# A two-layer hybrid trunk on one core: order of the gating work, place of the rotary tables, split scaling of probabilities, and the last transposes of a gating group

## The chip, the cores and the metric

The kernel runs on one core of one Trainium2 chip. The metric is device time in microseconds (us) for one execution; the median over several runs counts, and lower is better. TensorE multiplies matrices, VectorE (DVE in the profile) and ScalarE (ACT) do elementwise work, GpSimd (POOL) does elementwise work too and issues some transfers, and SyncE (SP) issues most transfers.

## The reference

The reference is a decoder trunk over 1024 tokens of width 1024, in float32, with two layers:

- Layer 0 mixes tokens with latent attention: a down projection to 704 columns (384 for queries, 256 for keys and values, 64 for a shared rotary key), norms, 8 heads with a plain part of 128 and a rotary part of 64, causal softmax, an output projection.
- Layer 1 mixes tokens with a chunked gating unit: `z = gelu(hn @ w_in)` is cut into halves u and v of 2048 columns; v gets a layer norm; within each block of 128 tokens and each of 8 groups of 256 columns, `sv = tril(w_s) @ v + b_s`; then `y = u * sv` and the mixer returns `y @ w_out`.
- After each mixer comes a feed-forward part (width 4096, squared relu) and a gated input embedding, both added to the residual stream.

## The kernel before

**Numbers.** Each float32 operand X of a product is split into a rounded part Xh (a copy, on ACT) and the rest Xl = X - Xh (on DVE); a product is Wh*Xh + Wh*Xl + Wl*Xh, three matmuls that accumulate in PSUM. `split` (L110 to L112) makes such a pair. Every matmul of the helper `mm` is recorded at L65.

**Order.** The program is written as one stream. A planner at build time turns it into one queue for each engine: it goes through a model of the engines' times and, where an engine is free in the model and the next instruction of the program is not ready in it, takes a later one that is. On the chip each queue then runs in its fixed order, and an instruction that must wait holds up all that stand behind it on its engine. `tc.issue_after(ins)` keeps the instructions of a block behind `ins` on the same engine.

**Start (L1002 to L1319).** x comes in blocks of 128 tokens. `block_x` transposes a block on TensorE; `block_lat` multiplies it by the down weights, eight k steps of six matmuls, and the first two blocks run interleaved. The weights arrive by transfer, one slice for each k; `down_weight(k)` makes their rounded part on ACT (L1065) and the rest on DVE (L1066) just before step k of block 0. At the end of block 0 (L1130) `rotary()` calls `rope_tables` (L1461 to L1490): six DVE instructions reduce the angles (L1468 to L1472), ACT forms a magnitude and two sines (L1475 to L1477) behind a load of another function table, DVE forms the sine and cosine tables from them (three instructions at L1478 to L1480, eight at L1486 to L1489), and ACT loads the table of logarithm and exponential again (L1288). `rotary()` then also transposes the remaining gains (L1289) and forms one product of gains (L1290). After block_lat, ACT squares the latent rows (L1136), `rsqrt_small` takes reciprocal roots behind the table load, DVE scales the rows into `lats` (L1141 to L1143), and `block_c` transposes `lats` on TensorE (L1151, tile `cp`).

**Attention (L1321 to L1458).** The work is cut into 32 units, a head and a pair of query blocks. `scores` (L1348) computes a row block of n = 128 to 1024 keys, DVE finds the maximum, ACT the exponentials with their sum (L1373), DVE the reciprocal (L1375), and POOL multiplies the n probabilities by it in one instruction (L1376). `turn_p` (L1379) transposes the probabilities in groups of 256 keys (L1388 to L1393, tile `pt`), and `values` (L1399) multiplies them with the values.

**Gating unit (L782 to L928).** First all v columns are computed, their statistics taken, and v parked in memory. Then four groups `gp` of 512 columns follow. In a group, for each of the 8 token blocks b: `unit(b)` computes u (24 matmuls, tile `up`) and ACT applies gelu; `prep(b)` brings v back in pairs of blocks (tile `vr`, one of four buffers shared with weights), normalizes it on DVE (L884), multiplies and adds the norm's gains on POOL (L885, L886) and splits it into `vhl`, of which there is one buffer in a group; `spatial(b)` multiplies by the spatial weights (tile `sv`) and DVE forms y in place of u (L908, two instructions); `turn_y(b)` transposes y (L914, tile `yp`) and splits it into `yh`, `yl`. The loop at L918 runs spatial(b-2), unit(b), prep(b-1), turn_y(b-2). Then `down_slice` (L656) multiplies the group's y by its 512 rows of `w_out` (tile `go`) and adds to the residual stream (L665). With `seq=True` its first output tile (j = 0) is computed for tokens 0 to 511 first and for tokens 512 to 1023 after; the others alternate between the two halves. Block 7 is in the second half.

## Time and profile before

| | |
|---|---|
| median of 3 runs | 2653.01 us (2651.12 to 2656.77) |
| the profiled execution, its own time | 2655.07 us |
| its span, first to last instruction | 2653.3 us |
| mean granted TensorE clock | 0.995 |
| DVE busy | 1480.3 us (56%) |
| ACT busy | 1040.1 us (39%) |
| POOL busy | 322.8 us (12%) |

The profile gives, for each engine, its busy time; views of it list which instructions an engine waited for and how long, the instructions in order of time, groups of equal instructions, and the granted clock of a stretch. "Idle before" an instruction is the time in which its engine did nothing just before it, with the instruction whose end ended it.

### The profile page before, as it was taken

What the parts mean: (1) busy time and instruction counts of PE and PEld (TensorE: products, weight loads), DVE (VectorE), ACT (ScalarE), POOL (GpSimd) and SP (SyncE); (2) the same over time, 40 slices, a digit from 0 to 9 for tenths busy, and PEclk for the clock granted to TensorE, in tenths of its full rate; (3) what the DMA queues carried; (4) which work ended last, traced back from release to release, by engine and by line L of the source; (5) the groups of instructions that cost most, each with busy time, mean ns of one, the idle gap of its engine ahead of it and who ended that gap; (6) DMA issues with size and microseconds to landing.
All of it is one profiled execution on the core that took longest, in us unless ns stands there. A gap on an engine that the chain in (4) does not pass through costs nothing. (4 is left out here: it accounts for less than half of the span.)

```text
span 2653.3 us, 33181 instructions
## 1 busy us (share of the span) xinstructions
PE 2595.6 (98%) x12736; PEld 2193.9 (83%) x12736; DVE 1480.3 (56%) x2396; ACT 1040.1 (39%) x2109; POOL 322.8 (12%) x460
## 2 busy tenths in 40 slices
PE   7999999999999999999999999999999999999999
PEld 7988888878888888888888787888788888888887
DVE  5677775886565434375522545336966654444641
ACT  4576773654443212164522312214644441221430
POOL 4544431000000000001211433030000000000000
PEclk9999999999999999999999999999999999999999
DMA  5200002233345323233232312212333362332220
GB/s 163 71 8 21 25 25 88 96 119 104 127 151 190 115 68 111 64 100 90 86 111 95 101 39 88 77 43 96 98 125 111 120 228 97 112 111 64 80 76 36
DMA packets 211341, 247.41 MB, mean 93 GB/s; under 512 B 9792, under 2 KB 159872, under 8 KB 211184
## 3 DMA queue, kind: packets, MB, share of 16 engines
q1 hardware_dynamic: 206368, 230.21, 26.9%
q0 software_dynamic: 4816, 15.10, 1.9%
q8 instruction: 100, 1.64, 0.3%
q14 instruction: 57, 0.47, 0.1%
HBM read 186.55 MB, written 58.72 MB: 92 GB/s over the span
## 5 line engine op out<-in xcount | busy, mean ns | idle before, releaser
L111 ACT CAST wh<-raw 128x1024 fp32r<-128x1024 f32 x96 | 100.9, 1051 | 390.8 <-PE f0d L65 130.3
L665 DVE TENSOR_TENSOR f0h<-f0d,f0h 128x512 f32<-128x512 f32 (+1 forms) x84 | 70.4, 866 | 166.0 <-PE f0d L65 166.0
L665 DVE TENSOR_TENSOR f1h<-f1d,f1h 128x512 f32<-128x512 f32 (+1 forms) x84 | 70.4, 865 | 157.5 <-PE f1d L65 157.5
L112 DVE TENSOR_TENSOR wl<-raw,wh 128x1024 fp32r<-128x1024 f32 x96 | 117.8, 1227 | 56.5 <-ACT wh L111 50.3
L744 POOL TENSOR_TENSOR f0h<-sig,f0h 128x512 f32<-128x512 f32 x16 | 21.9, 1388 | 846.1 <-DVE sig L743 827.4
L65 PE MATMUL go<-yl,wh 128*128 128x512 f32 x256 | 84.3, 395 | 2.7 <-DVE yl L112 2.7
L824 DVE BATCH_NORM_STATS2 vst<-vg 128x6 f32<-128x512 f32 (+1 forms) x40 | 23.3, 586 | 113.5 <-ACT vg L823 113.4
L65 PE MATMUL go<-yh,wh 128*128 128x512 f32 x256 | 84.6, 395 | 0.0
L65 PE MATMUL go<-yh,wl 128*128 128x512 f32 x256 | 83.3, 392 | 0.0
L894 ACT ACTIVATE u<-up,n_r 128x512 f32<-128x512 f32 x32 | 22.0, 687 | 155.4 <-PE up L65 155.2
L665 DVE TENSOR_TENSOR f0h<-go,f0h 128x512 f32<-128x512 f32 (+1 forms) x52 | 40.4, 809 | 63.6 <-PE go L65 63.6
L65 PE MATMUL s<-kT,q 128*128 128x512 f32 (+5 forms) x288 | 72.8, 355 | 2.4 <-DVE q L112 1.8
L823 ACT ACTIVATE vg<-vp,n_r 128x512 f32<-128x512 f32 (+1 forms) x40 | 24.0, 603 | 122.9 <-PE vp L65 121.5
L65 PE MATMUL av<-pt,v 128*128 128x256 f32 (+1 forms) x480 | 64.1, 284 | 5.2 <-DVE sm L1375 2.7
L65 PEld LDWEIGHTS av<-pt,v 128*128 128x128 f32 x480 | 59.9, 191 | 8.1 <-issue 3.7
L1376 POOL TENSOR_SCALAR p<-p,sm 128x128 f32<-128x128 f32 (+3 forms) x64 | 49.2, 770 | 86.8 <-DVE sm L1375 55.3
L65 PEld LDWEIGHTS go<-yl,wh 128*128 128x128 f32 x256 | 48.4, 189 | 13.3 <-DVE yl L112 3.8
L65 PE MATMUL f1d<-f_ah,wh 128*128 128x512 f32 x192 | 59.3, 390 | 0.0
L65 PE MATMUL f0d<-f_ah,wh 128*128 128x512 f32 x192 | 59.2, 390 | 0.0
L65 PE MATMUL f0d<-f_al,wh 128*128 128x512 f32 x192 | 59.2, 389 | 0.0
L65 PE MATMUL f1d<-f_al,wh 128*128 128x512 f32 x192 | 59.2, 389 | 0.0
L65 PE MATMUL f1d<-f_ah,wl 128*128 128x512 f32 x192 | 59.1, 389 | 0.0
(5412 smaller groups left out, 8029.2 us busy)
## 6 DMA issues: line engine op xcount, KB each, us to landing
raw<-in_ffn_w_down_dram SPq DMA_DIRECT2D x56, 512.0 KB, 3.6
f0ar<-f_apark SPq DMA_DIRECT2D x32, 512.0 KB, 3.5
f1ar<-f_apark SPq DMA_DIRECT2D x32, 512.0 KB, 3.4
raw<-in_ffn_w_down_dram SPq DMA_DIRECT2D x32, 256.0 KB, 3.0
raw<-in_ple_w_gate_dram SPq DMA_DIRECT2D x16, 512.0 KB, 4.1
vr<-vpark SPq DMA_DIRECT2D x16, 512.0 KB, 4.4
raw<-in_gmlp_w_out_dram SPq DMA_DIRECT2D x16, 512.0 KB, 3.5
vpark<-vg POOLq DMA_DIRECT2D x24, 256.0 KB, 2.3
```

What stands on the lines that cost most here:

```text
L65: PE.matmul(o, l, r, start=start, stop=stop)
L111: S.copy(hi, src)
L112: V.tensor_tensor(lo, src, f32(hi), op=ALU.subtract)
L665: V.tensor_tensor(h[j][:, c], u, h[j][:, c], op=ALU.add)
L744: G.tensor_tensor(h[j][:, cs], sg, h[j][:, cs], op=ALU.add)
L823: last = S.activation(t, o, AF.Gelu_apprx_tanh, scale=nrm.r[:, b:b + 1])
L824: V.bn_stats(vst[:, b, cc], t)
L894: S.activation(us[b][:, b % 2], o, AF.Gelu_apprx_tanh, scale=r[:, b:b + 1])
L1376: G.tensor_scalar(pr_[:, :n], pr_[:, :n], sm[:, 2:3], 1.0, op0=ALU.mult, op1=ALU.mult)
```

## The change

Four things change.

- **Gating order.** The normalization of v (L884) of block b is kept, on DVE, behind the second half of the split of block b-2 (of block 0 where b is 1), and that of block 0 behind the last split of y of the group before.
- **The last y transposes.** `turn_y(7)` leaves the loop. `down_slice` computes its first two output tiles together in the new `gemm_pair`: both for tokens 0 to 511, then both for tokens 512 to 1023; the four transposes of block 7 are put behind matmul 21 of the 24 of the first half, and kept behind it on TensorE.
- **Rotary tables.** `rotary()` is called at step k = 1 of block 0 rather than k = 7; the transposition of the gains stays at k = 7 as `later_gains()`.
- **Probabilities.** The POOL instruction at L1376 becomes two where n is over 512: columns 0 to 511, and the rest.

```diff
-        PE.matmul(o, l, r, start=start, stop=stop)
+        return PE.matmul(o, l, r, start=start, stop=stop).ins
...
     def split(hi, lo, src):
         S.copy(hi, src)
-        V.tensor_tensor(lo, src, f32(hi), op=ALU.subtract)
+        return V.tensor_tensor(lo, src, f32(hi), op=ALU.subtract).ins
+    @contextmanager
+    def behind(ins):
+        if ins is None:
+            yield
+        else:
+            with tc.issue_after(ins):
+                yield
     def load_block(w, k0, f0, nk=4, nf=256):
         cnt[0] += 1
...
                 for c in cset:
                     mm(acc[c], wl, rhs[k][c][0], False, k == nk - 1)
         return units
+    def gemm_pair(blocks, rhs, name, mid=None):
+        full = psg(f"{name}0")
+        acc = [[full[:, CS[c]] for c in range(2)], [pso(f"{name}1_{c}") for c in range(2)]]
+        w = [(hi[:, kk], lo[:, kk]) for hi, lo in blocks for kk in range(hi.shape[1])]
+        for c in range(2):
+            for f in range(2):
+                fs = slice(f * P, (f + 1) * P)
+                for k, (wh, wl) in enumerate(w):
+                    mm(acc[f][c], wh[:, fs], rhs[k][c][0], k == 0, False)
+                    mm(acc[f][c], wh[:, fs], rhs[k][c][1], False, False)
+                    last = mm(acc[f][c], wl[:, fs], rhs[k][c][0], False, k == len(w) - 1)
+                    if mid is not None and (c, f, k) == (0, 1, 2):
+                        mid(last)
+        return {f: [(acc[f][c], CS[c]) for c in range(2)] for f in range(2)}
     def chunked(hi, lo, n):
         return [[(hi[:, k, CS[c]], lo[:, k, CS[c]]) for c in range(2)] for k in range(n)]
...
                 down_sweeps(down, 4 * s, cur, h, f"f{i}d{s}", nxt, late)
         return h
-    def down_slice(w, k0, rhs, h, name, nxt, seq=False, before=None, after=None):
+    def down_slice(w, k0, rhs, h, name, nxt, seq=False, before=None, after=None, mid=None):
         bl = None
         for q in range(4):
             bl, ahead = bl or [load_block(w, k0, q * 256)], None
+            units = {}
+            if seq and q == 0:
+                units = gemm_pair(bl, rhs, name, mid)
             for f in range(2):
                 j = 2 * q + f
                 if before is not None:
                     before(j)
-                for u, c in gemm(bl, rhs, f, f"{name}{j}", seq and j == 0):
+                for u, c in units.get(f) or gemm(bl, rhs, f, f"{name}{j}"):
                     V.tensor_tensor(h[j][:, c], u, h[j][:, c], op=ALU.add)
                 if nxt is not None and f == 0 and q < 3:
                     ahead = [load_block(w, k0, (q + 1) * 256)]
...
             V.bn_aggr(mv[:, b], vst[:, b])
         rs = rsqrt_small(mv[:, :, 1], EPS, "lnr")
+        y_last = [None]
         for gp in range(4):
             f0 = gp * 512
             gb = tmp(f"gb{gp}", [P, 2, 512])
...
                 w = [t for part in load_cols(w_in, f0, f"wu{gp}", "x") for t in part]
             yh, yl = (pa.tile([P, 4, T], F32R, tag="a", name=f"y{x}{gp}") for x in "hl")
             vhl = tmp(f"vhl{gp}", [P, 2, 512], F32R)
-            us, vr = {}, {}
+            us, vr, done = {}, {}, {}
             def prep(b):
                 if b % 2 == 0:
                     vr[0] = pr.tile([P, 2, 512], F32, tag="raw", name=f"vr{gp}{b}")
                     nc.sync.dma_start(vr[0], vpark[b:b + 2, :, f0:f0 + 512].rearrange("b p f -> p b f"))
                 v = vr[0][:, b % 2]
-                V.tensor_scalar(v, v, mv[:, b, 0:1], rs[:, b:b + 1], op0=ALU.subtract, op1=ALU.mult)
+                with behind(y_last[0] if b == 0 else done.get(0 if b == 1 else b - 2)):
+                    V.tensor_scalar(v, v, mv[:, b, 0:1], rs[:, b:b + 1], op0=ALU.subtract, op1=ALU.mult)
                 G.tensor_tensor(v, v, gb[:, 0], op=ALU.mult)
                 G.tensor_tensor(v, v, gb[:, 1], op=ALU.add)
-                split(vhl[:, 0], vhl[:, 1], v)
+                done[b] = split(vhl[:, 0], vhl[:, 1], v)
             def unit(b):
                 o = pso(f"up{gp}{b}")
...
                     es = slice(e * 256, (e + 1) * 256)
                     V.scalar_tensor_tensor(u[:, es], o[:, es], bst[:, g:g + 1], u[:, es], op0=ALU.add, op1=ALU.mult)
-            def turn_y(b):
+            def turn_y(b, ins=None):
                 u = us.pop(b)[:, b % 2]
                 pp = pso(f"yp{gp}{b}")
-                for j in range(4):
-                    PE.transpose(pp[:, j * P:(j + 1) * P], u[:, j * P:(j + 1) * P], idf)
+                with behind(ins):
+                    for j in range(4):
+                        PE.transpose(pp[:, j * P:(j + 1) * P], u[:, j * P:(j + 1) * P], idf)
                 bs = slice(b * P, (b + 1) * P)
-                split(yh[:, :, bs], yl[:, :, bs], pp.rearrange("p (j t) -> p j t", t=P))
+                y_last[0] = split(yh[:, :, bs], yl[:, :, bs], pp.rearrange("p (j t) -> p j t", t=P))
             for b in range(NB + 2):
                 if b >= 2:
...
                     unit(b)
                 if 1 <= b <= NB:
                     prep(b - 1)
-                if b >= 2:
+                if 2 <= b <= NB:
                     turn_y(b - 2)
             down_slice(w_out, 4 * gp, chunked(yh, yl, 4), h, f"go{gp}", nxt if gp == 3 else None, seq=True,
-                       after=after if gp == 3 else None)
+                       after=after if gp == 3 else None, mid=lambda ins: turn_y(NB - 1, ins))
     def ple_out(i, h, nrm):
...
                     mm(B, xl[:, k], wh[:, QL:], False, en)
                     if k == 6 and b in late_x:
                         square_x(b, *late_x[b])
+                    if k == 1 and b == 0:
+                        rotary()
                     if k == KT - 1 and b == 0:
-                        rotary()
+                        later_gains()
                     yield
                 ss = const.tile([P, 4], F32, tag="ssl", name=f"ssl{b}", bufs=2)
                 lat = tmp(f"lats{b}")
...
             def rotary():
                 with tc.issue_after(rope_tables(tab, pos, gq, inv).ins):
                     table.append(S.preload_act_table_set(LNEXP))
+            def later_gains():
                 gains_turn(*gb, 16)
                 V.scalar_tensor_tensor(gqk, gT[:, 48:49], SCALE, gT[:, 49:50], op0=ALU.mult, op1=ALU.mult)
...
                     S.activation(pr_[:, :n].rearrange("p (c x) -> p c x", c=ns), sv, AF.Exp,
                                  bias=sm[:, 0:1], accum_out=sm[:, 1:2])
                     V.reciprocal(sm[:, 2:3], sm[:, 1:2])
-                    G.tensor_scalar(pr_[:, :n], pr_[:, :n], sm[:, 2:3], 1.0, op0=ALU.mult, op1=ALU.mult)
+                    for c0, c1 in ((0, min(n, 512)), (512, n)):
+                        if c1 > c0:
+                            G.tensor_scalar(pr_[:, c0:c1], pr_[:, c0:c1], sm[:, 2:3], 1.0, op0=ALU.mult, op1=ALU.mult)
                     prob[hd, j] = pr_
             def turn_p(hd, p, groups):
```

## Rows read from the trace of the kernel before

**Rows 1.** The page, part 1: busy us (share of the span) and instructions, all engines.
```profile
PE 2595.6 (98%) x12736; PEld 2193.9 (83%) x12736; DVE 1480.3 (56%) x2396; ACT 1040.1 (39%) x2109; POOL 322.8 (12%) x460
```

**Rows 2.** The waits of TensorE: instruction, releaser, us in total, times, longest us.
```profile
PE pt L1388 <- POOL p L1376: 4.6, 6, 1.0
PE yp L914 <- DVE u L908: 4.6, 3, 1.8
PE sv L65 <- DVE vhl L112: 4.4, 1, 4.4
PE cp L1151 <- ACT lats L1136: 4.2, 1, 4.2
PE go L65 <- DVE yl L112: 2.7, 2, 1.4
PE lat L65 <- ACT wdh L1065: 2.5, 1, 2.5
```

**Rows 3.** Windows behind four waits: stretch, us, PE busy, granted clock, DMA share, GB/s.
```profile
39.00:44.00 5.00, 5.00 (x20) 0.52 0.44 131
228.00:232.00 4.00, 4.00 (x23) 0.57 0.01 2
1477.00:1481.00 4.00, 4.00 (x14) 0.57 0.06 14
1525.00:1529.00 4.00, 4.00 (x14) 0.57 0.41 150
```

**Rows 4.** Timeline of DVE, start of the first gating group: start us, us, instruction, idle before.
```profile
1465.31 9.53 DVE L884 TENSOR_SCALAR vr<-vr,mv,lnrr 128x512 f32<-128x512 f32 x8
1474.77 1.74 DVE L112 TENSOR_TENSOR vhl<-vr,vhl 128x512 fp32r<-128x512 f32 x1
```

**Rows 5.** Groups of POOL by form: line, tile, shape, count, busy us, mean ns.
```profile
L885 POOL TENSOR_TENSOR vr<-vr,gb 128x512 f32<-128x512 f32 x32 | 46.8, 1478 | 90.2 <-DVE vr L884 90.2
...
L1376 POOL TENSOR_SCALAR p<-p,sm 128x1024 f32<-128x1024 f32 x8 | 9.0, 1122 | 14.1 <-DVE sm L1375 12.4 <-PE s L65 1.7
...
L1376 POOL TENSOR_SCALAR p<-p,sm 128x512 f32<-128x512 f32 x8 | 5.8, 729 | 6.7 <-DVE sm L1375 6.7
```

**Rows 6.** Timeline of ACT, split of the last y of the second group.
```profile
1625.24 0.59 ACT L111 CAST yh<-yp 128x512 fp32r<-128x512 f32 x1 [2.75 <-PE yp L914]
```

**Rows 7.** Timeline of TensorE, end of the second group's gating.
```profile
1624.31 0.44 PE L914 MATMUL yp<-idf,u 128*128 128x128 f32 x2 [1.35 <-DVE u L908]
...
1628.47 0.50 PE L65 MATMUL go<-yl,wh 128*128 128x512 f32 x1 [1.40 <-DVE yl L112]
```

**Rows 8.** Timeline of DVE, the same stretch.
```profile
1627.27 0.55 DVE L884 TENSOR_SCALAR vr<-vr,mv,lnrr 128x512 f32<-128x512 f32 x1 [2.62 <-DMA vr<-vpark]
1627.73 0.68 DVE L112 TENSOR_TENSOR yl<-yp,yh 128x512 fp32r<-128x512 f32 x1
```

**Rows 9.** Windows: one turn of the gating loop, transposes to transposes; columns as in rows 3.
```profile
1484.35:1490.95 6.60, 6.60 (x35) 1.00 0.24 79
```

**Rows 10.** Timeline of DVE, normalization inside the first group's output product.
```profile
1541.54 1.00 DVE L884 TENSOR_SCALAR vr<-vr,mv,lnrr 128x512 f32<-128x512 f32 x2
```

**Rows 11.** Timeline of TensorE, change from one head to the next.
```profile
227.60 0.33 PE L1388 MATMUL pt<-idf,p 128*128 128x128 f32 x1 [1.03 <-POOL p L1376]
```

**Rows 12.** Timeline of ACT, first two blocks.
```profile
17.50 3.20 ACT L1065 ACTIVATE wdh<-wdraw,gT 128x704 fp32r<-128x704 f32 x4 [1.80 <-DMA wdraw<-in_mla_w_down_dram]
...
28.23 0.42 ACT L1475 ACTIVATE rw<-rw 128x256 f32<-128x256 f32 x1 [5.71 <-DVE rw L1472]
...
30.79 1.28 ACT L1288 ACT_TABLE_LOAD   x1
32.09 0.49 ACT L1136 ACTIVATE lats<-lat 128x384 f32<-128x384 f32 x1
```

**Rows 13.** Timeline of DVE, first two blocks.
```profile
12.52 0.17 DVE L1300 COPY pos<-posp 128x8 f32<-128x8 f32 x1 [0.65 <-PE posp L1298]
...
30.41 0.43 DVE L1478 TENSOR_TENSOR rw<-rw 128x256 f32<-128x256 f32 x1 [2.21 <-ACT rw L1476]
```

More of the change, by code (lines that the diff above doesn't have):

```diff
@@ L1 @@
-from contextlib import ExitStack
+from contextlib import ExitStack, contextmanager
 import concourse.bass as bass
```

## The prediction

> **What bounds the kernel now.** The page comes first: TensorE is busy 2595.6 of 2653.3 us [rows 1]. The change removes no matmul and no transpose, so what it can win lies in TensorE's 58 us of idle time and in the stretches in which its clock is low. The second view is therefore TensorE's waits [rows 2]: the reader sees who ended each. Five of them belong to lines that the change touches: probabilities from POOL (4.6 us, 6 times), y from DVE's gating (4.6 us, 3 times), the split v (4.4 us, once), the first latent rows (4.2 us, once), the last split y (2.7 us, twice). The third view is the windows behind four of these waits [rows 3]: TensorE is busy all the time there, at a granted clock of 0.52 to 0.57, mostly the lower of its two levels (1.2 and 2.4 GHz). So a wait costs its own length and, in these four cases, more: 5 us x 0.48 = 2.4 us behind the wait for latent rows, and 4 us x 0.43 = 1.7 us behind each of the other three. Not every wait is followed by a low clock: behind the second and third group ends I found full clock.
>
> **The sum, part by part.** It is made against the profiled execution, 2655.07 us, which is 2.06 us above the median of 2653.01.
>
> *First gating group.* All eight normalizations stand in a row on DVE from 1465.31 and take 9.53 us; the split of block 0, for which TensorE waits, begins only at 1474.77 [rows 4]. In the new order only block 0's normalization stands ahead of that split. Its chain is then 1.2 us (9.53 / 8) of DVE, two POOL instructions of about 1.48 [rows 5], 0.6 us of ACT (a cast of this size [rows 6]) and DVE's split, at most 1.74: 6.5 us from 1465.31, or 1471.8. The wait of 4.4 us ended at about 1476.6, so it began at 1472.2. The split arrives just in time: -4.4 us of wait and -1.7 of low clock, **-6.1**. What is late next is nothing of this group: block 1 is needed one loop turn later. The bounds are 0 (another order on POOL) and -6.1.
>
> *Ends of the groups.* The end of the second group shows both waits. The transposes of block 7 wait 1.35 us for the gating [rows 7]. Then DVE comes to the next group's first normalization, stands 2.62 us until its transfer lands, and only at 1627.73 makes the second half of y's split [rows 8], whose rounded half ACT had begun at 1625.24 [rows 6]; TensorE waits 1.40 us [rows 7]. The change puts all 21 matmuls of the first half that are not needed as cover ahead of the transposes, and the normalization behind the split. That removes 4.6 + 2.7 = 7.3 us and, at the first group, 1.7 of low clock. What is added: one turn of the gating loop takes 6.6 us for 24 matmuls of 512 columns, six of 256 and four of 128 [rows 9], so one of 512 takes 0.236 us. Behind the transposes stand only three, or 0.7 us, and then the second half asks for block 7. ACT needs 0.6 us and DVE 0.7 for the split [rows 6, 8], with handoffs some 1.5 us. The remainder is 0.8 us in each of four groups if the planner finds no cover, and 0 if it moves later tiles' first halves up, as it does now. I take 0.5: +2.0. Sum: **-7.0**, bounds -9.0 and -5.8. The normalization now waits behind the split, and what queues behind it on DVE are additions to the residual stream, whose PSUM buffers are not needed for several us. The normalizations that ran inside the output product (two in 1.00 us [rows 10]) move into the gating stage; POOL's 3 us a block [rows 5] fit in a turn of 6.6 us. `gemm_pair` issues the same 48 matmuls as before, and the transfers keep their order: 0.
>
> *Probabilities.* Four of the six waits, 0.9 to 1.04 us each, stand where one head follows another, behind an instruction of 1024 columns; one is at 227.60 [rows 11]. A piece of 512 takes 0.729 us against 1.122 for the whole [rows 5], so the first transposes go 0.39 us earlier: 4 x 0.39 = **-1.6**. The other two waits are for rows of at most 512 columns. The second piece ends 2 x 0.729 - 1.122 = 0.34 us later than the whole did, 32 times: 11 us of POOL, hidden by POOL's idle time (322.8 us busy of 2653 [rows 1]) and by the first piece's transposes, which come before. If that cover were gone it would cost up to 11 us. Bounds +1.4 (if the transposes waited for both pieces) and -3.3 (if the low clock at 228 goes too).
>
> *Rotary tables.* At present ACT idles until 28.23 for the angles, then loads, takes sines and loads again until 32.09 [rows 12]; only then do the squares of block 0 begin, and TensorE waits 4.2 us for its rows. With the tables made early this block's rows are ready when TensorE gets there: -4.2 and -2.4 of low clock. But the 3.86 us on ACT must go somewhere. The positions are there at 12.7, and six DVE instructions of at most 0.43 follow a weight split, so the angles are ready near 16.2 [rows 13] and ACT's part would end near 20. At 17.50 ACT begins four weight casts, as soon as their transfers land [rows 12], and TensorE already waits 2.5 us for one of them [rows 2]. If the sines stand ahead, the casts come 2.5 us later, all of it paid; if behind, nothing. After that DVE has eleven instructions, at most 11 x 0.43 = 4.7 us [rows 13], between the weight splits: 0 if they fit between (a k step of both blocks, 4224 columns, keeps TensorE 1.9 us at the rate of [rows 9]), all 4.7 if they go ahead. I take +2.5, the nearest row. Sum **-4.1**, bounds -6.6 and +0.6. The gains' transposition keeps its place: 0.
>
> The table load shows 1.28 us, and ACT's next instruction starts 0.02 us after it [rows 12]. The Trainium skill (ScalarE: Activation LUTs, What ACT_TABLE_LOAD costs) counts 2.66 us for every switch, a drain included. By that the casts would come another 2.8 us later (2 x 1.38) and the sum of this part would be an estimated -1.3; the measured row decides.
>
> Total: -6.1 - 7.0 - 1.6 - 4.1 = -18.8 us, so 2636.3 for an execution like the profiled one and **2634.2** against the median. I give 2634.5.
>
> **The rivals.**
>
> *Everything hides (0.14).* No remainder at the group ends, the sines behind the casts, the low clock at 228 gone: -6.1 - 9.0 - 3.3 - 6.6 = -25.0, or 2628. For it: the waits at the group ends count three and two [rows 2], and the fourth group's end has none.
>
> *The tables displace the weight casts (0.17).* The shift of 2.5 + 4.7 us on ACT and DVE is paid in full and only half of the wait for latent rows and its low clock goes (-3.3): this part costs +3.9, the total is -10.8, 2642. For it: TensorE already waits for a cast there. Against it: DVE idles between the splits.
>
> *The queue order was not the cause (0.09).* Data come as late as before: the first gating split is held by POOL, the group ends get new waits as long as the old, and only about 3 us are won in all: 2650, no change by the bound below. Against it: DVE, not POOL, is at the wrong work when TensorE waits [rows 4, 8].
>
> *The gating becomes a chain in series (0.06).* With one `vhl` buffer and block b's normalization kept behind the split of block b-2, a block could cost more than the turn of 6.6 us [rows 9]. The normalization takes 1.19 us beside POOL's work [rows 4] but 0.50 where I saw POOL start only after it [rows 10], so the two engines hold each other up, and now they meet in every block. One block alone takes the 6.5 us worked out above; it decides from 6.6 us on. At 7.5 us, 0.9 x 31 blocks = 28 us lost against 18.8 won: 2662, slower. Against it: two blocks may be in flight. The Trainium skill (SBUF — State Buffer, Who interferes with whom) says the port pair that both use is held for a whole instruction, and the other engine blocks. By that rule the split too may wait for a whole POOL instruction, which would make a block 6.5 + 1.5 = 8.0 us and the time an estimated 2678. The row agrees that far: the split took 1.74 us beside POOL [rows 4] and 0.68 for the same number of columns without it [rows 8].
>
> **How the numbers follow.** A measurement of this kernel can tell 0.2%, 5.3 us, from no change. The forecast has 0.54, with its own range 2630 to 2639. Faster: forecast, everything hides, displaced casts: 0.54 + 0.14 + 0.17 = 0.85. Same: 0.09. Slower: 0.06. The range 2627 to 2646 holds the three faster cases with their bounds and leaves out the last two and a little of the tails.
>
> **What would show it.** In the profile after: no wait of TensorE for the split v at 1472; the DVE queue of the first group with one normalization before the first split; no DVE idle for a transfer between block 7's gating and its split; TensorE's wait for probabilities near 0.6 us where heads change; no wait at the first `cp`, and the wait for weight casts at 17 grown by about 2.5 us. Full clock behind 1477 and 1525. I am wrong if TensorE's idle time shrinks by less than 8 us, if a wait for v's split comes back in every block, or if the wait for casts grows by more than 6 us.

## The result, and the profile after

The changed kernel takes 2632.22 us (median of 4 runs, 2631.53 to 2633.76), the kernel before 2652.68 beside it (2651.12 to 2656.77). The ratio is 0.9919 with a 95% interval of 0.9907 to 0.9932: faster by 0.8%, or 20.5 us. The forecast was 2634.5 us, with a range of 2627 to 2646. The profiled execution took 2631.87 us, 0.35 below its median, with a span of 2629.9; that of the kernel before lay 2.4 above the median measured here. So the two traces differ by 23.4 us of span and the medians by 20.5, and some 2.7 us of what the traces show belongs to the two executions and not to the change.

The page of the changed kernel, part 1 (busy us, share, instructions), answers to [rows 1]:

```profile
PE 2587.3 (98%) x12736; PEld 2186.2 (83%) x12736; DVE 1463.6 (56%) x2396; ACT 1039.4 (40%) x2109; POOL 322.1 (12%) x492
```

TensorE's idle time is 2629.9 - 2587.3 = 42.6 us, where it was 57.7. That is 15.1 us; its busy time fell by another 8.3 with the same number of instructions, and the mean granted clock rose from 0.995 to 0.998. POOL has 32 instructions more, the second pieces. The waits of TensorE (instruction, releaser, us in total, times, longest) answer to [rows 2]:

```profile
PE xp L1120 <- DMA x<-in_x_dram: 4.4, 2, 2.5
PE lat L65 <- ACT wdh L1097: 3.5, 1, 3.5
...
PE pt L1426 <- POOL p L1414: 2.5, 5, 0.6
PE cp L1185 <- ACT lats L1170: 2.4, 1, 2.4
```

The waits for the split v, for the gating and for the last split y (4.4, 4.6 and 2.7 us) are no longer in the list. The wait for probabilities fell from 4.6 to 2.5 us, that for the first latent rows from 4.2 to 2.4; the one for weight casts grew from 2.5 to 3.5. Equal instructions in the two traces show where the time came from: the last transposition of latent rows at the start (tile `cq`) is 2.8 us earlier, the last score product 6.0, the tile `gtok` ahead of the gating unit 6.4, and the first product of the feed-forward part behind it (`f1u0g`) 22.0. So the start gave 2.8, attention 3.2, the gating unit 15.6, and the rest of the program 1.8.

**First gating group.** DVE's timeline (start, us, instruction, idle before) has one normalization where [rows 4] had eight in a row:

```profile
1458.90 0.55 DVE L915 TENSOR_SCALAR vr<-vr,mv,lnrr 128x512 f32<-128x512 f32 x1
1462.87 0.69 DVE L112 TENSOR_TENSOR vhl<-vr,vhl 128x512 fp32r<-128x512 f32 x1 [3.42 <-ACT vhl L111]
```

Block 0 is normalized by itself, POOL needs two instructions of 1.29 us, and the split follows at 1462.87. TensorE's timeline has no bracket before the product that needs it, which starts right behind the last product of `up`, 1.9 us after the split's end (1462.87 + 0.69):

```profile
1465.22 0.39 PE L65 MATMUL up<-wu0h,n_30l 128*128 128x512 f32 x1
1465.45 0.40 PE L65 MATMUL sv<-vhl,wsh 128*128 128x256 f32 x2
```

The windows behind the first group's start and its end (stretch, us, PE busy, granted clock, DMA share, GB/s) show full clock where [rows 3] showed 0.57:

```profile
1465.00:1469.00 4.00, 4.00 (x22) 1.00 0.01 2
1515.00:1519.00 4.00, 4.00 (x19) 1.00 0.01 4
```

**End of the second group.** TensorE's timeline, answering to [rows 7]:

```profile
1608.84 0.60 PE L946 MATMUL yp<-idf,u 128*128 128x128 f32 x4
...
1609.96 1.12 PE L65 MATMUL go<-yh,wh 128*128 128x512 f32 x4
1610.92 0.42 PE L65 MATMUL go<-yl,wh 128*128 128x512 f32 x1
```

The transposes of block 7 stand without a wait at 1608.84. Behind them come the three matmuls that were left of the first half, and then, in the row at 1609.96, four that need rounded y alone: by the queue's order two belong to the next output tile and one to each of the two second halves. The first product with `yl` of block 7 follows at 1610.92 without a wait. DVE's timeline answers to [rows 8]:

```profile
1610.09 0.69 DVE L112 TENSOR_TENSOR yl<-yp,yh 128x512 fp32r<-128x512 f32 x1 [1.19 <-ACT yh L111]
1610.70 0.68 DVE L694 TENSOR_TENSOR f0h<-go,f0h 128x512 f32<-128x512 f32 x1
1611.75 0.55 DVE L915 TENSOR_SCALAR vr<-vr,mv,lnrr 128x512 f32<-128x512 f32 x1 [0.38 <-DMA vr<-vpark]
```

The second half of the split comes first, an addition second, and the normalization last. It still waits for its transfer (0.38 us), but no wait of TensorE came of it.

**Start.** ACT's timeline (columns as before), answering to [rows 12]:

```profile
17.46 2.43 ACT L1097 ACTIVATE wdh<-wdraw,gT 128x704 fp32r<-128x704 f32 x3 [0.73 <-DMA wdraw<-in_mla_w_down_dram]
...
26.12 0.42 ACT L1513 ACTIVATE rw<-rw 128x256 f32<-128x256 f32 x1 [3.65 <-DVE rw L1510]
26.55 1.28 ACT L1514 ACT_TABLE_LOAD   x1
27.85 0.42 ACT L1514 ACTIVATE rw<-rw 128x256 f32<-128x256 f32 x1
```

The casts at 17.46 are not displaced. The sines wait for the angles until 26.12, ten microseconds later than the forecast's 16.2. Two rows of DVE show instructions that last far longer than their size explains, the second on three columns:

```profile
21.08 2.60 DVE L1510 SCALAR_TENSOR_TENSOR rw<-rw 128x256 f32<-128x256 f32 x1
...
32.83 1.76 DVE L1534 TENSOR_SCALAR rl0v<-ssl,v 128x3 f32<-128x3 f32 x1
```

and two rows of POOL show what runs beside them, its sum of x of 1024 columns:

```profile
21.01 2.39 POOL L1141 TENSOR_TENSOR xs<-xh,xl 128x1024 f32<-128x1024 f32 x1 [13.27 <-ACT xs L1140]
...
32.17 2.39 POOL L1141 TENSOR_TENSOR xs<-xh,xl 128x1024 f32<-128x1024 f32 x1 [7.53 <-ACT xs L1140]
```

The instruction on three columns ends at 34.59, 0.03 us after POOL's (32.17 + 2.39 = 34.56). It is the first step of the reciprocal root that block 0's rows need; TensorE waits for these rows until 36.44:

```profile
36.44 1.08 PE L1185 MATMUL cp<-idf,lats 128*128 128x128 f32 x4 [2.38 <-ACT lats L1170]
```

### The profile page after: what moved, and what is told of

The parts are those of the page before. It is cut to its first block, busy times and chain, and to the rows that moved or that the text cites. A ratio compares the mean times of both kernels' runs of the same rounds, so it can differ in the third digit from the quotient of the medians.

```text
span 2629.9 us, 33196 instructions
## 1 busy us (share of the span) xinstructions
PE 2587.3 (98%) x12736; PEld 2186.2 (83%) x12736; DVE 1463.6 (56%) x2396; ACT 1039.4 (40%) x2109; POOL 322.1 (12%) x492
## 4 chain that ended last, share of the span: by engine, by line
PE 85%; DVE 6%; ACT 4%; issue 1%; DMA 0%; POOL 0%; ACTq 0%; DVEq 0%; POOLq 0%
PE f0d L65 13%; PE f1d L65 12%; PE vp L65 7%; PE up L65 7%; PE go L65 6%; PE e L65 4%; PE wo L65 3%; PE pg L65 3%; PE s L65 2%; PE pq L65 1%; PE av L65 1%; PE sv L65 1%; PE pj L65 1%; PE f1u3g L419 1%; PE f0u3g L419 1%; PE f0u10g L419 1%
## 5 line engine op out<-in xcount | busy, mean ns | idle before, releaser
L916 POOL TENSOR_TENSOR vr<-vr,gb 128x512 f32<-128x512 f32 x32 | 42.0, 1317 | 242.1 <-DVE vr L915 242.1
L1414 POOL TENSOR_SCALAR p<-p,sm 128x512 f32<-128x512 f32 (+2 forms) x96 | 56.9, 601 | 82.3 <-DVE sm L1411 51.4
L65 PE MATMUL f0d<-f_ah,wl 128*128 128x512 f32 x192 | 59.1, 389 | 0.0
```

Source lines behind the costliest of these rows:

```text
L65: return PE.matmul(o, l, r, start=start, stop=stop).ins
L916: G.tensor_tensor(v, v, gb[:, 0], op=ALU.mult)
L1414: G.tensor_scalar(pr_[:, c0:c1], pr_[:, c0:c1], sm[:, 2:3], 1.0, op0=ALU.mult, op1=ALU.mult)
```

## The experiments

Times against the kernel before go with its median in the same set of runs (2652.53, 2652.59 and 2653.00); times against the changed kernel go with its 2632.22. These come from different sets, whose medians of the kernel before differ by up to 0.5 us.

### Each part alone

**The gating order alone.** The edit is the `behind` line at the normalization with its two records, on the kernel before.

```diff
+                with behind(y_last[0] if b == 0 else done.get(0 if b == 1 else b - 2)):
+                    V.tensor_scalar(v, v, mv[:, b, 0:1], rs[:, b:b + 1], op0=ALU.subtract, op1=ALU.mult)
-                split(vhl[:, 0], vhl[:, 1], v)
+                done[b] = split(vhl[:, 0], vhl[:, 1], v)
...
+                y_last[0] = split(yh[:, :, bs], yl[:, :, bs], pp.rearrange("p (j t) -> p j t", t=P))
```

> The kernel before with the gating order alone: block b's normalization stays on DVE behind the split of block b-2, block 0's behind the last split of y. Theory (DVE did the wrong work while TensorE waited): the wait for v's split at 1472 goes (4.4 us and 1.7 us of low clock behind it, 6.1) and the two waits of the output product for the last split y (2.7 us) go too, so about -8.8 us, 2644; the waits of the y transposes for the gating (4.6 us) stay. Rival (POOL's two instructions, not DVE's order, set when the split comes): the wait at 1472 stays above 3 us and the time within 3 us of the kernel before.

Measured: 2642.95 us, ratio 0.9965 (0.9951 to 0.9978), -9.6 us. No wait for the split v and none for the last split y is left; the first two waits of TensorE's list are:

```profile
PE pt L1398 <- POOL p L1386: 4.6, 6, 1.0
PE yp L924 <- DVE u L918: 4.6, 3, 1.6
```

The wait of the transposes for the gating stays, at 4.6 us. So the order on DVE, not POOL, held both splits. The theory gave 8.8; the low clock behind the first group's end went as well (granted clock 1.00 from 1517 to 1525), though the transposes still wait 1.6 us there.

**The transposes inside the output product alone.** The edit is `gemm_pair` and the call of `turn_y(NB - 1)` from it; order, tables and probabilities as before.

> The kernel before with the pairing of the first two output tiles alone, the four transposes of block 7 behind matmul 21 of the first half; the other three edits undone. Theory: the 4.6 us in which the y transposes wait for the gating go, with the 1.7 us of low clock behind the first group's end, so about -6.3 us, 2646.5; the wait for v's split (4.4) stays, and the output product still waits for the last split y (2.7 us or more), since the next group's normalization still stands ahead of it on DVE. Rival (the wait only changes its place, since the split comes as late as before): the waits of the output product for y grow by as much as those of the transposes shrink, and the time stays within 3 us of the kernel before.

Measured: 2649.94 us, ratio 0.9987 (0.9979 to 0.9996), -2.6 us. The rival was right here. The waits of the transposes are gone, and those of the output product for the split y grew from 2.7 to 5.5:

```profile
PE go L65 <- DVE yl L112: 5.5, 3, 2.1
```

DVE's timeline at the second group's end shows why:

```profile
1623.46 1.00 DVE L914 TENSOR_SCALAR vr<-vr,mv,lnrr 128x512 f32<-128x512 f32 x2 [2.89 <-DMA vr<-vpark]
1624.38 0.68 DVE L112 TENSOR_TENSOR yl<-yp,yh 128x512 fp32r<-128x512 f32 x1
```

The normalizations of the next group still stand ahead of the split and wait 2.89 us for their transfer, as in [rows 8]. The pair of tiles brings TensorE to this split sooner, and it stands there instead; of the 4.6 us that the transposes no longer wait, the split takes back 2.8.

**The early tables alone.** The edit is the place of the call, with the gains left at k = 7.

```diff
+                    if k == 1 and b == 0:
+                        rotary()
                     if k == KT - 1 and b == 0:
-                        rotary()
+                        later_gains()
```

> The kernel before with the early rotary tables alone. By the trace of the changed kernel the matching instruction after the prologue comes 2.9 us earlier: about -2.9 us, 2650, with the wait for the first latent rows at 2.4 us and no longer wait for weight casts. Rival (the 2.9 us came from elsewhere, from another order that the planner chose): 0 here.

Measured: 2649.90 us, ratio 0.9990 (0.9981 to 0.9999), -2.6 us. The waits of the start:

```profile
PE gps L98 <- DMA grawb<-in_mla_k_nope_g_dram: 3.0, 1, 3.0
...
PE cp L1153 <- ACT lats L1138: 2.3, 1, 2.3
...
PE lat L65 <- ACT wdh L1065: 1.0, 1, 1.0
```

The wait for the rows is 2.3 us, as in the changed kernel, and that for casts 1.0. The waits of the start for transfers differ from run to run (a wait for gains shows here with 3.0 us), so the gain is better read from several profiles: the last `cq` stands at 105.4 to 107.8 us in the five that have the old start (the kernel before, the three others of "one part alone" or the two gating parts together) and at 102.4 to 104.5 in the four with the early tables and nothing else new at the start. The means are 106.6 and 103.4, a difference of 3.2 us.

**Two pieces of the probabilities alone.**

```diff
-                    G.tensor_scalar(pr_[:, :n], pr_[:, :n], sm[:, 2:3], 1.0, op0=ALU.mult, op1=ALU.mult)
+                    for c0, c1 in ((0, min(n, 512)), (512, n)):
+                        if c1 > c0:
+                            G.tensor_scalar(pr_[:, c0:c1], pr_[:, c0:c1], sm[:, 2:3], 1.0, op0=ALU.mult, op1=ALU.mult)
```

> The kernel before with POOL's scaling in two pieces alone. Theory: three waits where heads change fall from 1.0 to 0.6 us, the fourth goes, and the low clock behind 228 us with them: -2.9 us, 2650. Forecast as it was worked out: -1.6 us. Rival (the second piece's end, 0.34 us later in 32 units, delays the other transposes): 0 or slower by 1 to 2 us, with new waits for POOL in the middle of heads.

Measured: 2650.17 us, ratio 0.9991 (0.9982 to 1.0000), -2.4 us.

```profile
PE pt L1390 <- POOL p L1378: 2.5, 5, 0.6
```

The waits for probabilities are 2.5 us in all, the longest 0.6, as in the changed kernel. No new waits for a second piece show. The time lies between forecast and theory and can't tell them apart. The traces can: from the last `cq` to the last score product this kernel takes 302.6 us, and the three other parts alone 304.4 to 304.5, none of which shows the low clock at 228; so the pieces are worth 1.8 us, near the forecast.

### The two gating parts together

The four parts alone give 9.6 + 2.6 + 2.6 + 2.4 = 17.2 us, and all together gave 20.5. This run asks whether the difference lies between the two gating parts.

> The changed kernel without the early tables and without the two pieces: gating order and the transposes inside the output product, together. Theory (the pair of tiles takes away the wait for the gating only if the next group's normalization is no longer ahead of the split): the gating stage 15.6 us shorter than before, as in the changed kernel, 3 us more than the two edits measured alone (9.6 + 2.6): about 2637. Rival (the edits add up): -12.2 us, 2640.3.

Measured: 2637.34 us, ratio 0.9935 (0.9921 to 0.9948), -15.7 us. This is 3.5 us more than 9.6 + 2.6, as the theory has it; but each of the three differences is known to some 2 to 4 us only. The traces agree: from the first `gtok` to the first `f1u0g` the stage is 10.8 us shorter than before with the order alone, 1.5 with the pair alone and 15.5 with both, where the two kernels without a gating edit differ from before by up to 1.5. With it goes the mechanism that the pair alone showed, a wait that only changed its place. With the other two parts' 2.6 and 2.4 it makes 20.7 us, so the remaining parts add up.

### The two kinds of order

**Without the order inside a group.**

```diff
-                with behind(y_last[0] if b == 0 else done.get(0 if b == 1 else b - 2)):
+                with behind(y_last[0] if b == 0 else None):
```

> The changed kernel without the edges from block b's normalization to the split of block b-2; the edge of block 0's normalization to the last split of y stays. Theory (the first split waits because the planner puts all eight normalizations ahead of it): the wait for v's split comes back in the first group, 4.4 us and 1.7 of low clock, so +6 us against the changed kernel, 2638; the group ends stay without waits. Rival (other edits moved the normalizations anyway): 0.

Measured: 2643.12 us, ratio 0.9967 (0.9954 to 0.9979), +10.9 against the changed kernel. TensorE's wait for the split v is back:

```profile
1470.72 0.58 PE L65 MATMUL sv<-vhl,wsh 128*128 128x256 f32 x1 [4.43 <-DVE vhl L112]
```

That part was as expected. But waits for the last split y came back too, 2.9 us in three, which was not. DVE's timeline at the second group's end:

```profile
1620.08 0.55 DVE L915 TENSOR_SCALAR vr<-vr,mv,lnrr 128x512 f32<-128x512 f32 x1 [2.45 <-DMA vr<-vpark]
1620.54 0.68 DVE L112 TENSOR_TENSOR yl<-yp,yh 128x512 fp32r<-128x512 f32 x1
```

Block 0's normalization is kept behind the split; the one that waits 2.45 us ahead of it must be another block's, from the same pair of transferred blocks, which nothing kept back any more. One bound at the head of a row is not enough when the second of the row may overtake the first. The waits of 4.4 and 2.9 us are not the whole 10.9: the granted clock is 0.50 from 1470 to 1476, an estimated 2.6 us (half of the 5.3 us that TensorE is busy there) where 1.7 was expected. The remaining 1.0 was not traced.

**Without the order at the group's end.**

```diff
-                with behind(y_last[0] if b == 0 else done.get(0 if b == 1 else b - 2)):
+                with behind(None if b == 0 else done.get(0 if b == 1 else b - 2)):
```

> The changed kernel without the edge of block 0's normalization to the last split of y; the edges inside a group stay. Theory (a normalization that stands for its transfer held the second half of the last split): waits of the output product for the split y come back at two group ends, +2.7 us against the changed kernel, 2635; the first group stays without its wait. Rival (with the pair of tiles as cover the split's delay is hidden): 0.

Measured: 2637.04 us, ratio 0.9941 (0.9928 to 0.9955), +4.8 against the changed kernel. The waits for the last split y are back:

```profile
PE go L65 <- DVE yl L112: 3.4, 3, 1.6
```

and DVE shows the same figure, a normalization that waits for its transfer ahead of the split:

```profile
1610.79 0.55 DVE L915 TENSOR_SCALAR vr<-vr,mv,lnrr 128x512 f32<-128x512 f32 x1 [2.51 <-DMA vr<-vpark]
1611.25 0.68 DVE L112 TENSOR_TENSOR yl<-yp,yh 128x512 fp32r<-128x512 f32 x1
```

The wait is 3.4 us and not 2.7, since TensorE now comes to the split sooner. In the trace the gating stage is 4.2 us longer than in the changed kernel; the rest of the 4.8 was not traced.

### The start: what holds DVE

**Squares kept back.** Block 1's squares on ACT, and the POOL sum that follows, are kept behind the exponential of block 0's reciprocal root.

```diff
-                        square_x(b, *late_x[b])
+                        with behind(exp0[0] if b == 1 else None):
+                            square_x(b, *late_x[b])
...
-        S.activation(r, r, AF.Exp, scale=-0.5)
+        last = S.activation(r, r, AF.Exp, scale=-0.5).ins
+        if keep is not None:
+            keep.append(last)
```

> The changed kernel with one thing more: block 1's squares of x on ACT, and with them POOL's sum of x that follows, are kept behind the exponential of block 0's reciprocal root. Theory (POOL's sum of 1024 columns, 2.4 us, holds up the instruction of DVE on three columns that the reciprocal root needs, 1.76 us where it should be some 0.1): the wait for the first latent rows falls from 2.4 to 0.6 us or less and the low clock behind it goes, -2 to -3 us against the changed kernel, 2630. Rival (the rows are late because the angles are, 10 us later than forecast; POOL is not in it): the wait stays at 2.4 us. Second rival: the squares come too late for block 1 and a new wait opens there, 0 or slower.

Measured: 2630.50 us (2629.59 to 2632.06), -1.7 against the changed kernel. DVE's instruction on three columns, and then TensorE's wait:

```profile
33.49 0.22 DVE L1536 TENSOR_SCALAR rl0v<-ssl,v 128x3 f32<-128x3 f32 x1
```

```profile
35.56 0.63 PE L1187 MATMUL cp<-idf,lats 128*128 128x128 f32 x4 [0.82 <-DVE lats L1177]
```

It takes 0.22 us where it took 1.76, and the wait is 0.82 us. The median is where the theory put it, but 1.7 us is less than can be told from no change; the rows are what decides. Of the 1.6 us by which the wait is shorter, 0.9 is the transposes' earlier start (35.56 against 36.44) and 0.7 a TensorE that came later. Against the first rival: the transposes began 0.9 us earlier though ACT took the angles 0.8 later (26.89 against 26.12). The hold itself moved on: an instruction on three columns for block 1, at 38.90, takes 2.46 us beside POOL's next sum, but TensorE does not wait for block 1's rows.

**POOL's sum in four pieces.**

```diff
-                G.tensor_tensor(xs, f32(xh).rearrange("p k t -> p (k t)"), f32(xl).rearrange("p k t -> p (k t)"), op=ALU.add)
+                for q in range(4):
+                    qs = slice(q * 256, (q + 1) * 256)
+                    G.tensor_tensor(xs[:, qs], f32(xh).rearrange("p k t -> p (k t)")[:, qs], f32(xl).rearrange("p k t -> p (k t)")[:, qs], op=ALU.add)
```

> The changed kernel with POOL's sum of x (1024 columns, 2.4 us) in four pieces of 256. Theory (DVE is held for as long as the POOL instruction that runs lasts): the instruction on three columns takes 0.7 us or less instead of 1.76, and the wait for the first latent rows falls by about 1 us. Rival (DVE waits until POOL has nothing left to do): 1.7 us or more as before, no gain.

Measured: 2631.46 us (2631.00 to 2631.90), -0.8. The same instruction of DVE, and POOL's pieces:

```profile
32.30 0.78 DVE L1536 TENSOR_SCALAR rl0v<-ssl,v 128x3 f32<-128x3 f32 x1
```

```profile
31.64 2.78 POOL L1143 TENSOR_TENSOR xs<-xh,xl 128x256 f32<-128x256 f32 x4 [5.93 <-ACT xs L1140]
```

A piece takes 0.70 us (2.78 / 4), so the second ends at 33.03, and DVE's instruction at 33.08. It began at 32.30, 0.03 us before the first piece's end, and stood until the second had ended. That is near the theory's 0.7 us, and it speaks for POOL rather than for ACT's squares, which the edit before moved too; but TensorE reached the rows' transposes earlier in this run and its wait for them is 3.0 us, not shorter.

**Both edits.**

> The changed kernel with block 1's squares of x kept behind the exponential of block 0's reciprocal root and POOL's sum of x in four pieces, the two edits together. Theory (both shorten the time for which POOL holds DVE's small instructions): the wait for the first latent rows at 0.8 us or less, no instruction on three columns over 0.8 us before 42 us, and the time at most that of either edit alone: 2629 to 2631 where the changed kernel gave 2632.2. Rival (one edit uses up the gain, and pieces add POOL's time per instruction): 2631 to 2632.

Measured: 2629.64 us (2628.84 to 2630.64), ratio 0.9908 (0.9894 to 0.9921) to the kernel before, -2.6 against the changed kernel, whose four runs all lie above these. Two expectations failed. The wait for the rows is 1.8 us:

```profile
35.34 0.63 PE L1189 MATMUL cp<-idf,lats 128*128 128x128 f32 x4 [1.83 <-DVE lats L1179]
```

The transposes begin at 35.3 us in this run and at 35.6 in that of the first edit; TensorE merely reaches them earlier here. And while block 0's instruction takes 0.21 us, one of block 1 still took 2.10, during the next sum in pieces:

```profile
39.18 2.10 DVE L1544 SCALAR_TENSOR_TENSOR rl1t<-rl1v,rl1t 128x3 f32<-128x3 f32 x1
```

```profile
39.12 2.82 POOL L1144 TENSOR_TENSOR xs<-xh,xl 128x256 f32<-128x256 f32 x4
```

**Probabilities in three pieces**, on top of both edits.

```diff
-                    for c0, c1 in ((0, min(n, 512)), (512, n)):
+                    for c0, c1 in ((0, min(n, 256)), (256, min(n, 512)), (512, n)):
```

> The same kernel with the probabilities scaled in three pieces (columns 0 to 255, 256 to 511, the rest) where n is over 512, and in two where it is over 256. Theory (a group of transposes waits only for the piece it reads): five waits of up to 0.6 us shrink by about 0.25 us each, -1 us. Rival (the second piece now ends later than the first group of transposes, by some 0.3 us): as many new waits for the second piece, 0 or +1 us.

Measured: 2629.38 us (2628.76 to 2629.72), 0.3 less than without. Two waits are shorter and one is longer:

```profile
PE pt L1430 <- POOL p L1418: 1.9, 5, 0.5
...
PE av L65 <- DVE sm L1415: 1.7, 3, 1.0
...
PE pt L1430 <- DVE q L112: 0.9, 1, 0.9
```

Against the kernel without the third piece, the wait for POOL fell from 2.5 to 1.9 us and that of the values from 2.4 to 1.7; those of the same transposes for DVE grew from 0.3 to 0.9, with smaller ones beside it (in all from 0.9 to 2.5). What is late next is DVE's work, and not the second piece as the rival had it. The gain was taken back by a new wait; this kernel and the one before it are the fastest of those run.

**Angles ahead of the weight splits**, on top of both edits.

```diff
-            V.scalar_tensor_tensor(a, b, -cst, a, op0=ALU.mult, op1=ALU.add)
+            angle.append(V.scalar_tensor_tensor(a, b, -cst, a, op0=ALU.mult, op1=ALU.add).ins)
...
+                with behind(angle[-1] if angle else None):
+                    V.scalar_tensor_tensor(lo, raw, g0[k], f32(hi), op0=ALU.mult, op1=ALU.subtract)
```

> The kernel with both edits of the start, and with the weight splits of steps 2 to 7 kept on DVE behind the last of the six angle instructions. Theory (the angles come 10 us later than forecast because the weight splits go between them): the angles are ready 5 us earlier or more and the wait for the first latent rows goes to 0, but weight splits and one cast of weights now stand behind the tables, and TensorE waits 2 to 5 us more for weights: the displacement that the prediction gave as a rival, 0 to +4 us in all. Rival (there is room on both engines): the weights come in time and the time falls by 1 us or more.

Measured: 2636.03 us (2635.58 to 2636.32), +6.4 against both edits alone. ACT's timeline, magnitude of the angles and a weight cast:

```profile
21.48 0.40 ACT L1520 ACTIVATE rw<-rw 128x256 f32<-128x256 f32 x1
...
25.32 0.88 ACT L1097 ACTIVATE wdh<-wdraw,gT 128x704 fp32r<-128x704 f32 x1
```

The magnitude is taken at 21.48 instead of 26.12, but a cast stands behind the sines until 25.32. TensorE's timeline:

```profile
29.12 0.59 PE L65 MATMUL lat<-wdl,xh 128*128 128x384 f32 x2 [3.87 <-DVE wdl L1099]
...
40.23 0.63 PE L1190 MATMUL cp<-idf,lats 128*128 128x128 f32 x4 [0.30 <-DVE lats L1180]
```

The rows come almost in time (0.30 us), and TensorE waits 3.87 us for a weight split that stands on DVE behind the tables. In this run, then, work was displaced, as the theory had it, at a higher price than expected (0 to +4). The angles were not as early as they could be either: on DVE an instruction that waited 4.10 us for ACT's squares, until 20.06, stood ahead of the last two angle instructions. An order that has the angles ready near the forecast's 16.2 was not tried.

## Why the prediction was right, point by point

The forecast was -18.8 us and the medians show -20.5. The four steps, with what each measured:

- **First gating group, -6.1.** Right: no wait at the split, one normalization ahead of it, full clock. The split was ready 1.9 us early where 0.4 was worked out: from the normalization's start to the split's end it took 4.7 us, not 6.5. The split took 0.69 us instead of 1.74, the normalization 0.55 instead of 1.2, and each of POOL's two instructions 1.29 instead of 1.48, since the normalizations no longer ran beside POOL's work. The rival that the queue order was not the cause fell with the order alone (-9.6).
- **Ends of the groups, -7.0.** All waits went, and the term that was mis-sized is the remainder of +2.0: it measured 0, with no wait of the transposes or of the output product at any of the four ends. At the end shown this is because the planner put matmuls that need only rounded y, two of them from the next tile, behind the transposes ("0 if it moves later tiles' first halves up"). Without it the two gating steps make -15.1; the gating stage gave 15.6 in the trace and the two parts together 15.7. What the prediction did not say is that the parts depend on each other: the pair of tiles alone is worth 2.6 us and with the order 15.7 - 9.6 = 6.1.
- **Probabilities, -1.6.** Waits at head changes fell to 0.6 us as forecast, and the total by 2.1. Attention took 3.2 us less in the trace, but 1.4 of that is the low clock at 228 of the profiled execution before, which three other kernels with the same unsplit waits did not show (a fourth did, below). What is left, 1.8, is near the term, and the traces of the part alone give the same; -2.4 was measured for it, with an interval that reaches to no change.
- **Rotary tables, -4.1.** The sum was 0.9 to 1.5 us too large: the gain is 2.6 us by the part alone and 3.2 by the nine profiles. Its numbers were off in opposite ways, so that it is near is luck. The +2.5 for shifted casts measured 0: the casts come first ("if behind, nothing", as the text put it). The step that failed is "this block's rows are ready when TensorE gets there", worth -4.2 and -2.4: a wait of 2.4 us stayed, and behind it a granted clock of 0.50 from 36.4 to 39.0. Two things held the rows. The angles were to be ready near 16.2 and were ready at 26.1, because the weight splits go between the six instructions and one of these, at 21.08, stood for 2.60 us beside POOL. And the reciprocal root's first step stood for POOL's sum. That was so in the kernel before too, where it took 1.89 us and ended 0.03 after POOL's instruction:

```profile
34.45 1.89 DVE L1496 TENSOR_SCALAR rl0v<-ssl,v 128x3 f32<-128x3 f32 x1 [0.26 <-ACT lats L1136]
33.79 2.52 POOL L1109 TENSOR_TENSOR xs<-xh,xl 128x1024 f32<-128x1024 f32 x1 [7.57 <-ACT xs L1108]
```

So an estimated 1.7 of the 4.2 us (1.89 against 0.22 without POOL's sum) were not the tables' at all, which the prediction left out. How much of the remaining 2.4 is the angles' was not measured by itself.

The total is near the measured one in part because the errors have opposite signs: 2.0 us too little at the group ends, 0.9 to 1.5 too much at the start.

That the gating becomes a chain in series did not come about. Its premise, that DVE and POOL now meet in every block, was wrong: in the changed kernel all 32 normalizations take 0.53 to 0.55 us (up to 1.52 before), 28 of the 32 splits 0.67 to 0.69 and four 1.11 to 1.12, and TensorE waits for none. The order that was feared to chain the engines keeps them apart. The Trainium skill (SBUF — State Buffer, Who interferes with whom), on whose rule that rival's higher price rested, says that one engine gets the shared port pair for its whole instruction and the other blocks; the trace agrees at the start of the kernel (1.76 us, ending 0.03 after POOL's instruction). On the table switches the measured row decided rightly: the load took 1.28 us again and the next instruction began 0.02 later. The Trainium skill (ScalarE: Activation LUTs, What ACT_TABLE_LOAD costs) counts 2.66 us for a switch; these rows do not show the drain in it.

Of the announced signs, one failed in favour of the kernel (the wait for casts did not grow by 2.5 us; it grew by 1.0, in a run in which a wait for gains ahead of it had gone) and one against it (a wait at the first `cp`).

## What to carry to other kernels

An instruction that waits for a transfer must not stand, in an in-order queue, ahead of one for which the critical engine waits; keep it behind, and keep the whole row behind, not its first member alone. A cover that brings the critical engine to a wait sooner pays only once what it waits for also comes sooner: measure the two edits together before judging either. When work is moved early, work out who else uses the engine in between: here the moved chain was late by ten microseconds, and the one way tried of forcing it cost more than it gave.

## What the runs showed of the hardware

**A small instruction can stand until a large one of another engine has ended.** Three columns on DVE took 1.76 us beside POOL's sum (1.89 in the kernel before) and 0.22 without. Cutting POOL's instruction into pieces of 0.70 us bounded the delay in one run (0.78), but in another an instruction of DVE at 39.18 stood until 41.28, which is three pieces (39.12 + 3 x 0.705 = 41.24). So pieces are no sure bound; keeping the large instruction away freed the instruction that it was kept away from, both times (0.22 and 0.21). The Trainium skill (SBUF — State Buffer, Who interferes with whom) has the port pair held for a whole instruction; the hold at 39.18 outlasted two ends of POOL's instructions, and no run here shows why.

**The same wait does not always lower the clock.** The windows give stretch, us, PE busy, granted clock, DMA share and GB/s. In the attention stage two kernels have the same unsplit probabilities with the same total of 4.6 us of waits. The window from 200 to 240 us of the two gating parts together:

```profile
200.00:240.00 40.00, 36.91 (x258) 0.96 0.09 29
```

and of the gating order alone:

```profile
200.00:240.00 40.00, 36.83 (x269) 1.00 0.09 27
```

The kernel without the order inside a group, with its probabilities in two pieces, shows such a stretch elsewhere:

```profile
360.00:400.00 40.00, 37.63 (x257) 0.96 0.13 41
```

Executions of one kernel differ too: the eleven of the transposes inside the output product alone have mean granted clocks from 0.993 (span 2652.1 us) to 0.997 (2646.0 to 2649.2). Where in them the clock was low is not on record, since only one was traced. So the low clock behind a wait of this length shows in some traces and not in others, and a single trace may not be read as if every execution had it; 1.4 us of the difference between the traces before and after is of this kind.
